# One-hots of picked experts laid out token by token, made by small VectorE operations

## The chip, the cores and the metric

The kernel runs on one core of one Trainium2 chip. The time is the device time of one execution in microseconds; lower is better. The core's engines work side by side, each through a queue of its own in a fixed order: TensorE (PE; its weight loads are listed as PEld), VectorE (DVE), ScalarE (ACT), GpSimd (POOL), and SyncE (SP), which issues transfers.

## What is computed

The reference is a transformer block with a mixture of 16384 experts (PEER), followed by two layers of another block, for 256 tokens of width 1024. The change touches the experts alone:

```python
def one(xb):                                  # xb: 128 tokens x 1024
    q = (xb @ w_pq).reshape(PEER_BLOCK, PEER_HEADS, 2, PEER_DKH)
    s = jnp.einsum('thpd,hpkd->thpk', q, sub_keys).astype(jnp.float32)
    sv, si = lax.top_k(s, PEER_TOPK)
    cand = (sv[:, :, 0, :, None] + sv[:, :, 1, None, :]).reshape(PEER_BLOCK, PEER_HEADS, -1)
    cidx = (si[:, :, 0, :, None] * N_KEYS + si[:, :, 1, None, :]).reshape(PEER_BLOCK, PEER_HEADS, -1)
    best, pos = lax.top_k(cand, PEER_TOPK)
    eidx = jnp.take_along_axis(cidx, pos, axis=-1)
    g = jax.nn.softmax(best, axis=-1)
    act = jax.nn.gelu(jnp.einsum('thkd,td->thk', expert_u[eidx], xb).astype(jnp.float32), approximate=False)
    return jnp.einsum('thk,thkd->td', (g * act).astype(xb.dtype), expert_v[eidx])
```

An expert's number is a pair (i, j) of two numbers under 128. Each token picks 16 of them in each of 8 heads, so 128 pairs with a weight each.

## The kernel before

The kernel gathers nothing. It computes all 16384 experts for all tokens, one slice of 128 experts (all i of one j) at a time, and multiplies the result by the tokens' weights, which are zero nearly everywhere. `up(j, lo)` is such a slice: a raw weight tile of 128x1024 is loaded, ScalarE copies it into `wh` (line 289), the high part, VectorE subtracts to get `wl` (line 293), the low part, and 24 matmuls follow in `mm3` (lines 274 to 276): for each of 8 parts of the model width `wh` with the tokens' high part, `wh` with their low part, `wl` with their high part. The first two of each three need `wh` alone. In this stage `wh` and `wl` have two buffers each (`wtile`, line 306).

The weights become a table by one-hots. For one token, partition p holds its p-th pick; `oo` is 1 in the column of the pick's i, `ow` holds the pick's weight in the column of its j, and the matmul of `oo` and `ow` sums over picks into a 128x128 table of that token. The weight is scaled by `WS` and split into two f16 parts, h = 0 and 1, so each token takes two matmuls. `prepare(t0)` makes `oo` and `ow` for four tokens, a group; `group()` does their eight matmuls (through `mm`, line 279) into one PSUM bank; `drain()` (lines 929 to 935) multiplies the finished slices `H1`, `H2` by the table, and ScalarE stores the table where no slice has come yet (line 935). In the loop at the end of this part, 64 groups are spread over 82 slices (`GR`), a group is prepared one ahead (`PD`), and drained three later (`LAG`). Where tokens already have their table, the slice's gelu (line 976) is multiplied into it (line 977).

`oo`, `ow` and the small tiles `k1` share six buffers (tag `k2`). The order of instructions on each engine is set by a scheduler when the program is built; each engine then keeps it. `choose` ends with the transposes that bring the picks' indices (`IJ`) and weights (`W2`) to partitions, a column per token.

Of the kernel before, what the change touches and what calls it, by code (L numbers as in the profile page):

```python
# [9 lines left out]
F32 = mybir.dt.float32  # L10
F32R = mybir.dt.float32r
BF = mybir.dt.bfloat16
F16 = mybir.dt.float16
U32 = mybir.dt.uint32
AF = mybir.ActivationFunctionType
OP = mybir.AluOpType
# [3 lines left out]
P = 128  # L20
D = 1024
T = 256
# [10 lines left out]
WS = 16384.0  # L33
# [226 lines left out]
class Kern:  # L260
# [566 lines left out]
    def peer(self, ys, gb):  # L827


        nc, tc, I = self.nc, self.tc, self.I  # L830
        st = ExitStack()
        pool = st.enter_context(tc.tile_pool(name="pe", bufs=1, reuse_waits="tile"))
# [11 lines left out]
            nc.sync.dma_start(xs[:, i * 512:(i + 1) * 512], self.X[i])  # L844
        nt.close()
        self.xpool.close()
        IJ = pool.tile([P, 2, T], F16, name="IJ")
        W2 = pool.tile([P, 2, T], F16, name="W2")
        io32 = pool.tile([P, P], F32, name="io32")
        nc.sync.dma_start(io32, I["iota"])  # L850
        iota = pool.tile([P, P, 4], F16, name="iota")
        nc.vector.tensor_copy(iota, io32[:, :, None].to_broadcast([P, P, 4]))
        g1s = st.enter_context(tc.tile_pool(name="g1", bufs=1, reuse_waits="tile"))
        H1 = g1s.tile([P, NJ1, T], F32, name="H1")
        tk = ExitStack()
        tp = tk.enter_context(tc.tile_pool(name="tk", bufs=1, reuse_waits="tile"))
# [18 lines left out]
        def second():  # L875
            ch = self.choose(tp, SV, SI, IJ, W2)
            for hp in range(16):
                w = pre
                if hp:
                    w = self.wsplit(self.raw(I["w_pq"][hp // 2], hp % 2, KD), lo="pool" if hp in POOLQ else "dve")  # L880
                pq = self.bank()
                for k in range(KD):
                    self.mm3(pq[:, :T], w[:, k], hT[k], k == 0, k == KD - 1)
                q = tp.tile([P, T], F32, tag="pq", name="pq", bufs=2)
                nc.scalar.activation(q, pq[:, :T], AF.Copy)
                yield
                sc = self.bank()
                for b in range(2):
                    self.mm(sc[:, b * P:(b + 1) * P], q[:, b * P:(b + 1) * P], skey[:, hp])
                for b in range(2):  # L890
                    o = (hp % 2, hp // 2 * 2 + b)
                    self.top16(tp, sc[:, b * P:(b + 1) * P], SV[:, o[0], o[1]], SI[:, o[0], o[1]])
                if hp % 2:
                    yield
                    next(ch)
                if hp % 4 == 3:
                    yield
                    next(ch)
                    yield
                    next(ch)  # L900
            next(ch)
            self.rest = ch
# [22 lines left out]
        def drain():  # L925
            nonlocal toks
            pg, ts = pend.pop(0)
            pv = pg.rearrange("p (t j) -> p j t", t=4)
            nc.vector.scalar_tensor_tensor(H1[:, :, ts], pv[:, :NJ1], 1.0 / WS, H1[:, :, ts], op0=OP.mult, op1=OP.mult)
            m = cols - NJ1  # L930
            if m:
                nc.vector.scalar_tensor_tensor(H2[:, :m, ts], pv[:, NJ1:cols], 1.0 / WS, H2[:, :m, ts],
                                               op0=OP.mult, op1=OP.mult)
            if cols < NKEY:
                nc.scalar.activation(H2[:, m:, ts], pv[:, cols:], AF.Copy, scale=1.0 / WS)
            toks = ts.stop

        def prepare(t0):
            ts = slice(t0, t0 + 4)
            B = [P, P, 4]  # L940
            oo = pool.tile([P, 2, P, 4], F16, tag="k2", name="oo", bufs=6)
            ow = pool.tile([P, 2, P, 4], F16, tag="k2", name="ow", bufs=6)
            for i in (1, 0):
                nc.vector.tensor_tensor(oo[:, i], iota, IJ[:, i, None, ts].to_broadcast(B), op=OP.is_equal)  # L944
            for h in range(2):
                nc.gpsimd.tensor_tensor(ow[:, h], oo[:, 1], W2[:, h, None, ts].to_broadcast(B), op=OP.mult)  # L946
            ready.append((oo, ow, ts))

        def group():
            oo, ow, ts = ready.pop(0)  # L950
            pg = self.bank()
            for i in range(4):
                for h in range(2):
                    self.mm(pg[:, i * P:(i + 1) * P], oo[:, 0, :, i], ow[:, h, :, i], start=h == 0, stop=h == 1)
            pend.append((pg, ts))
            if len(pend) > LAG:
                drain()
# [11 lines left out]
        for j in range(NJ1, NKEY):  # L969
            while n < 64 and n * GR < (j + 1 - NJ1 - GD) * 64:  # L970
                prepare(4 * n)
                n += 1
            pa = up(j, "dve" if j % PLO else "pool")
            if toks:
                ga = K1([P, T], F32)
                nc.scalar.activation(ga[:, :toks], pa[:, :toks], AF.Gelu)
                nc.vector.tensor_tensor(Hj(j)[:, :toks], ga[:, :toks], Hj(j)[:, :toks], op=OP.mult)
            if toks < T:
                nc.scalar.activation(Hj(j)[:, toks:], pa[:, toks:], AF.Gelu)
            cols = j + 1  # L980
            while len(ready) > (PD if n < 64 else 0):
                group()
            if n == 64 and not ready and pend:
                drain()
            if toks == T and j >= NKEY - VP:
                part(order[len(parted)])
# [38 lines left out]

    def choose(self, tp, SV, SI, IJ, W2):

# [3 lines left out]
        nc = self.nc  # L1031
        n = 4 * TOPK
        io32 = tp.tile([P, TOPK, n], F16, name="io32")
# [6 lines left out]
        stairs, o = [], 0  # L1040
# [5 lines left out]
        for h in range(PH):  # L1046
            cand = tp.tile([P, 2, o], F32, tag="cand", name="cand", bufs=2)
            hb = slice(2 * h, 2 * h + 2)
            for a0, a1, w, at in stairs:
                B = [P, 2, a1 - a0, w]  # L1050
                v.tensor_tensor(cand[:, :, at:at + (a1 - a0) * w].rearrange("p b (a c) -> p b a c", c=w),
                                SV[:, 0, hb, a0:a1, None].to_broadcast(B),
                                SV[:, 1, hb, None, 0:w].to_broadcast(B), op=OP.add)
            for b in range(2):
# [11 lines left out]
            t, ab = T2("t", F32, 4), T2("ab", F16, 2)  # L1066
# [16 lines left out]
            eq = tp.tile([P, 2, TOPK, n], F16, tag="eq", name="eq", bufs=1)  # L1083
            B = [P, 2, TOPK, n]
            v.tensor_tensor(eq, ab[:, :, None, :].to_broadcast(B), io32[:, None].to_broadcast(B), op=OP.is_equal)
# [11 lines left out]
        B = [P, 2 * PH, TOPK]  # L1097
# [11 lines left out]
        for b in range(2):  # L1109
            pt = self.bank()  # L1110
            for i in range(3):
                nc.tensor.transpose(pt[:, i * P:(i + 1) * P], ijw[:, i, b].rearrange("p h k -> p (h k)"), self.ident)
            o = slice(b * P, (b + 1) * P)
            nc.scalar.activation(IJ[:, :, o], pt[:, :2 * P].rearrange("p (i t) -> p i t", i=2), AF.Copy)
            pw = pt[:, 2 * P:3 * P]
            hi = tp.tile([P, P], F32, tag="whi", name="whi", bufs=2)
            nc.scalar.activation(W2[:, 0, o], pw, AF.Copy, scale=WS)
            nc.scalar.activation(hi, W2[:, 0, o], AF.Copy)
            nc.vector.scalar_tensor_tensor(W2[:, 1, o], pw, WS, hi, op0=OP.mult, op1=OP.subtract)
        yield  # L1120

    def glanes(self, *gens):
# [910 lines left out]
```

## Time and profile before

| | |
|---|---|
| median of 3 runs | 1929.62 us (1929.02 to 1930.05) |
| profiled execution | 1928.68 us |
| its span in the trace | 1926.9 us |
| mean granted TensorE clock | 0.992 of full speed |
| TensorE busy | 1857.6 us (96%) |
| VectorE busy | 1323.7 us (69%) |
| ScalarE busy | 970.3 us (50%) |
| GpSimd busy | 328.4 us (17%) |

Busy time is the time in which an engine has at least one instruction at work. The span is the profiled execution from its first to its last instruction; 1.8 us of the execution lie around it.

### The profile page before, as it was taken

Reading aid. Unit: us, or ns where it says so; the run is one execution under the profiler, and the core shown is the slowest. Engines: PE = TensorE matmul, PEld = TensorE weight load, DVE = VectorE, ACT = ScalarE, POOL = GpSimd, SP = SyncE. Lnnn points to the kernel's source line nnn. Section 1 sums busy time; section 2 is a strip of 40 time slices with the busy share of each in tenths; the row PEclk is TensorE's granted clock in tenths of the full one; section 3 lists DMA queues with packets and bytes.
Section 4 is the critical chain, followed back from the end, with each engine's and each line's share of the span. In section 5 each row is a group of like instructions: output and inputs, shape, how many; then the busy total and the mean of one; then the engine's idle time right before and its main releaser. Section 6 shows DMA issues by size and latency. Waiting matters only on the chain.

```text
span 1926.9 us, 32835 instructions
## 1 busy us (share of the span) xinstructions
PE 1857.6 (96%) x12634; PEld 1648.3 (86%) x12634; DVE 1323.7 (69%) x2901; ACT 970.3 (50%) x1792; POOL 328.4 (17%) x247
## 2 busy tenths in 40 slices
PE   7999989999999999999999999998999999989998
PEld 6776579999999999888888779987999899879997
DVE  4536668998788887555555665677777656767785
ACT  4535444443444444544444546445666464556563
POOL 0000003324644442000000003320100033200000
PEclk9999989999999999999999999999999999999999
DMA  8732544553444444656555653422666334225571
GB/s 309 246 109 89 175 144 141 177 174 122 148 138 142 143 142 154 209 190 189 187 186 184 208 195 110 131 66 82 200 223 228 100 110 132 66 77 172 194 232 60
DMA packets 85101, 302.93 MB, mean 157 GB/s; under 512 B 10096, under 2 KB 10992, under 8 KB 84816
## 3 DMA queue, kind: packets, MB, share of 16 engines
q1 hardware_dynamic: 84944, 300.83, 47.9%
q8 instruction: 99, 1.62, 0.4%
q14 instruction: 58, 0.48, 0.1%
HBM read 298.56 MB, written 2.10 MB: 156 GB/s over the span
## 4 chain that ended last, share of the span: by engine, by line
PE 78%; DVE 15%; ACT 3%; DMA 2%; issue 2%; SPq 0%; POOLq 0%; DVEq 0%; POOL 0%; ACTq 0%
PE b L276 20%; PE b L274 20%; PE b L275 20%; PE b L279 15%; DVE wl L293 4%; DVE oo L944 1%; PE b L1158 1%; ACT wh L289 1%; DMA raw<-in_wv 1%; PE b L524 1%; PE b L1349 1%; DVE eq L1089 0%; DVE tm L1022 0%; DVE u L1978 0%; DVE jt L741 0%
## 5 line engine op out<-in xcount | busy, mean ns | idle before, releaser
L289 ACT ACTIVATE wh<-raw 128x1024 fp32r<-128x1024 f32 x457 | 483.9, 1061 | 562.7 <-PE b L275 265.5
L293 DVE TENSOR_TENSOR wl<-raw,wh 128x1024 fp32r<-128x1024 f32 x414 | 559.7, 1352 | 270.8 <-ACT wh L289 270.5
L276 PE MATMUL b<-r,wl 128*128 128x256 f32 (+1 forms) x1216 | 347.5, 286 | 12.4 <-DVE wl L293 12.4
L274 PE MATMUL b<-r,wh 128*128 128x256 f32 (+1 forms) x1216 | 351.1, 289 | 0.0
L275 PE MATMUL b<-r,wh 128*128 128x256 f32 x1152 | 322.5, 280 | 0.0
L274 PE MATMUL b<-hh,wh 128*128 128x256 f32 x1056 | 301.6, 286 | 1.8 <-DVE ast L1674 1.8
L276 PE MATMUL b<-hh,wl 128*128 128x256 f32 x1056 | 299.7, 284 | 1.8 <-DVE wl L293 1.7
L275 PE MATMUL b<-hl,wh 128*128 128x256 f32 x1056 | 298.6, 283 | 0.0
L293 POOL TENSOR_TENSOR wl<-raw,wh 128x1024 fp32r<-128x1024 f32 x43 | 105.4, 2452 | 941.0 <-ACT wh L289 668.9
L276 PEld LDWEIGHTS b<-r,wl 128*128 128x128 f32 x1216 | 230.1, 189 | 21.3 <-DVE wl L293 19.8
L274 PEld LDWEIGHTS b<-r,wh 128*128 128x128 f32 x1216 | 231.2, 190 | 3.2 <-issue 1.5
L275 PEld LDWEIGHTS b<-r,wh 128*128 128x128 f32 x1152 | 218.3, 189 | 0.0
L274 PEld LDWEIGHTS b<-hh,wh 128*128 128x128 f32 x1056 | 202.2, 192 | 4.5 <-DVE ast L1674 2.3
L276 PEld LDWEIGHTS b<-hh,wl 128*128 128x128 f32 x1056 | 202.2, 191 | 3.1 <-DVE wl L293 3.0
L275 PEld LDWEIGHTS b<-hl,wh 128*128 128x128 f32 x1056 | 202.3, 192 | 1.4
L275 PE MATMUL b<-wl,k 128*128 128x512 f32 x492 | 195.0, 396 | 1.5 <-DVE wl L293 1.5
L274 PE MATMUL b<-wh,k 128*128 128x512 f32 x492 | 194.8, 396 | 0.0
L276 PE MATMUL b<-wh,k 128*128 128x512 f32 x492 | 194.6, 395 | 0.0
L946 POOL TENSOR_TENSOR ow<-oo,W 128x512 f16<-128x512 f16 x128 | 152.1, 1210 | 161.7 <-DVE oo L944 93.4
L275 PEld LDWEIGHTS b<-wl,k 128*128 128x128 f32 x492 | 92.4, 188 | 25.3 <-DVE wl L293 3.1
L1981 POOL TENSOR_TENSOR u<-u 128x256 f32<-128x256 f32 x44 | 33.6, 765 | 461.0 <-DVE u L1978 297.8
L274 PEld LDWEIGHTS b<-wh,k 128*128 128x128 f32 x492 | 92.4, 188 | 22.6 <-ACT wh L289 0.4
(491 smaller groups left out, 3150.4 us busy)
## 6 DMA issues: line engine op xcount, KB each, us to landing
raw<-in_eu SPq DMA_DIRECT2D x128, 512.0 KB, 3.9
raw<-in_ev SPq DMA_DIRECT2D x128, 512.0 KB, 3.6
raw<-in_fi SPq DMA_DIRECT2D x88, 512.0 KB, 4.5
raw<-in_w_ada SPq DMA_DIRECT2D x48, 512.0 KB, 5.3
raw<-in_wi SPq DMA_DIRECT2D x48, 512.0 KB, 3.9
raw<-in_fo SPq DMA_DIRECT2D x44, 512.0 KB, 4.6
raw<-in_w SPq DMA_DIRECT2D x16, 512.0 KB, 5.9
raw<-in_w_pq SPq DMA_DIRECT2D x16, 512.0 KB, 4.3
```

Source lines behind the costliest of these rows:

```text
L274: mm(out, L.hi, R.hi, start=start, stop=False, skip_group_check=True)
L275: mm(out, L.hi, R.lo, start=False, stop=False, skip_group_check=True)
L276: self.lastmm = mm(out, L.lo, R.hi, start=False, stop=stop, skip_group_check=True)
L279: self.nc.tensor.matmul(out, l, r, start=start, stop=stop, skip_group_check=True)
L289: nc.scalar.activation(dst.hi, src, AF.Copy)
L293: e.tensor_tensor(dst.lo, src, dst.hi.bitcast(F32), op=OP.subtract)
L524: nc.tensor.matmul(pa[32 * j:32 * j + 32, :P], self.s2[:, 4 * h + k], wa[:, k, m * P:(m + 1) * P], start=(k == 0), stop=(k == 3), tile_pos ...
L944: nc.vector.tensor_tensor(oo[:, i], iota, IJ[:, i, None, ts].to_broadcast(B), op=OP.is_equal)
L946: nc.gpsimd.tensor_tensor(ow[:, h], oo[:, 1], W2[:, h, None, ts].to_broadcast(B), op=OP.mult)
L1158: nc.tensor.matmul(pa[32 * j:32 * j + 32], self.s2[:, k], wa[:, j % 2 * 512:(j % 2 + 1) * 512], start=(k == 0), stop=(k == KD - 1), tile_p ...
L1349: nc.tensor.transpose(pt[:, sc * P:(sc + 1) * P], Pm[:, sc * P:(sc + 1) * P], self.ident)
L1981: nc.gpsimd.tensor_tensor(u[:, 0], u[:, 0], u[:, 1], op=OP.mult)
```

## The change

`oo` and `ow` are laid out token by token: the 128 columns of one token are neighbours, where before the four tokens of a group alternated. `oo` then holds the one-hot of i alone. `ow` is made straight from the column numbers in one operation with two per-partition scalars (equal to j, times the weight), where before a one-hot of j was made on VectorE and multiplied on GpSimd. Each operation covers one token, so a group takes 4 + 8 operations of 128 elements on VectorE, and none on GpSimd. `IJ` and `W2` become f32, and `iota` loses its factor of four.

```diff
-        IJ = pool.tile([P, 2, T], F16, name="IJ")
-        W2 = pool.tile([P, 2, T], F16, name="W2")
+        IJ = pool.tile([P, 2, T], F32, name="IJ")
+        W2 = pool.tile([P, 2, T], F32, name="W2")
...
-        iota = pool.tile([P, P, 4], F16, name="iota")
-        nc.vector.tensor_copy(iota, io32[:, :, None].to_broadcast([P, P, 4]))
+        iota = pool.tile([P, P], F16, name="iota")
+        nc.vector.tensor_copy(iota, io32)
...
         def prepare(t0):
             ts = slice(t0, t0 + 4)
-            B = [P, P, 4]
-            oo = pool.tile([P, 2, P, 4], F16, tag="k2", name="oo", bufs=6)
-            ow = pool.tile([P, 2, P, 4], F16, tag="k2", name="ow", bufs=6)
-            for i in (1, 0):
-                nc.vector.tensor_tensor(oo[:, i], iota, IJ[:, i, None, ts].to_broadcast(B), op=OP.is_equal)
-            for h in range(2):
-                nc.gpsimd.tensor_tensor(ow[:, h], oo[:, 1], W2[:, h, None, ts].to_broadcast(B), op=OP.mult)
+            oo = pool.tile([P, 4, P], F16, tag="k2", name="oo", bufs=6)
+            ow = pool.tile([P, 4, 2, P], F16, tag="k2", name="ow", bufs=6)
+            for i in range(4):
+                t = slice(t0 + i, t0 + i + 1)
+                nc.vector.tensor_scalar(oo[:, i], iota, IJ[:, 0, t], None, op0=OP.is_equal)
+                for h in range(2):
+                    nc.vector.tensor_scalar(ow[:, i, h], iota, IJ[:, 1, t], W2[:, h, t], op0=OP.is_equal, op1=OP.mult)
             ready.append((oo, ow, ts))
...
-                    self.mm(pg[:, i * P:(i + 1) * P], oo[:, 0, :, i], ow[:, h, :, i], start=h == 0, stop=h == 1)
+                    self.mm(pg[:, i * P:(i + 1) * P], oo[:, i], ow[:, i, h], start=h == 0, stop=h == 1)
...
-            hi = tp.tile([P, P], F32, tag="whi", name="whi", bufs=2)
-            nc.scalar.activation(W2[:, 0, o], pw, AF.Copy, scale=WS)
-            nc.scalar.activation(hi, W2[:, 0, o], AF.Copy)
-            nc.vector.scalar_tensor_tensor(W2[:, 1, o], pw, WS, hi, op0=OP.mult, op1=OP.subtract)
+            hi = tp.tile([P, P], F16, tag="whi", name="whi", bufs=2)
+            nc.scalar.activation(hi, pw, AF.Copy, scale=WS)
+            nc.scalar.activation(W2[:, 0, o], hi, AF.Copy)
+            nc.vector.scalar_tensor_tensor(W2[:, 1, o], pw, WS, W2[:, 0, o], op0=OP.mult, op1=OP.subtract)
```

The scheduler orders the changed program anew. On TensorE before, in the middle of the loop, with buffer numbers in the names (a slice has one `b`, `wh` and `wl`; `r` holds the tokens): the slice `b_6740` ends, the eight matmuls of a group follow, then the slice `b_6787` from its first matmul on.

```order
L276 MATMUL b_6740<-r_2441,wl_6737 128x256
L279 LDWEIGHTS oo_6675 [waits Activation_49]
L279 MATMUL b_6769<-ow_6676,oo_6675 128x128 [waits Pool_49]
...
L274 MATMUL b_6787<-r_2434,wh_6783 128x256 [waits Activation_49]
L275 MATMUL b_6787<-r_2434,wh_6783 128x256
L276 MATMUL b_6787<-r_2434,wl_6784 128x256 [waits DVE_49]
L274 MATMUL b_6787<-r_2435,wh_6783 128x256
```

On TensorE in the changed program, at the like place: the slice `b_6717` ends and a group follows; then come the first two matmuls of `b_6825`, the slice after next, and behind them the next slice, `b_6778`, whose own first two stand ahead of that group already.

```order
L276 MATMUL b_6717<-r_2441,wl_6714 128x256
L279 LDWEIGHTS oo_6697 [waits PE_49,DVE_49]
L279 MATMUL b_6807<-ow_6698,oo_6697 128x128 [waits Activation_49]
...
L274 MATMUL b_6825<-r_2434,wh_6821 128x256 [waits Activation_49]
L275 MATMUL b_6825<-r_2434,wh_6821 128x256
L276 MATMUL b_6778<-r_2434,wl_6775 128x256 [waits DVE_49]
L274 MATMUL b_6778<-r_2435,wh_6774 128x256
```

So two matmuls of each slice have moved ahead of the last 22 of the slice before it.

On ScalarE in the changed program, around the copy `wh_6821` that those two matmuls read: it waits for TensorE, and the gelu of the slice `b_6717` and the drain's store come behind it. The kinds stand in the same order as before the change.

```order
L935 ACTIVATE H2_4843<-b_6467 128x58x4 [waits DVE_49]
L289 ACTIVATE wh_6821<-raw_6819 128x1024 [waits DMAHW0_49,PE_49,Activation_49]
L976 ACTIVATE k1_6742<-b_6717 128x92 [waits PE_49,Activation_49]
L979 ACTIVATE H2_4843<-b_6717 128x164
L935 ACTIVATE H2_4843<-b_6528 128x57x4 [waits DVE_49]
```

On VectorE in the changed program, the same stretch: between two splits now stand the twelve small operations of a group, with L977 and L932 among them, where before two operations of L944 stood.

```order
L293 TENSOR_TENSOR wl_6775<-raw_6772,wh_6774 128x1024 [waits DMAHW7_49,DVE_49,PE_49]
L944 TENSOR_SCALAR oo_6758<-iota_2622,IJ_2618 128x128 [waits PE_49]
L977 TENSOR_TENSOR H2_4843<-k1_6742,H2_4843 128x92 [waits Activation_49]
L932 SCALAR_TENSOR_TENSOR H2_4843<-b_6528,H2_4843 128x35x4 [waits Activation_49]
L946 TENSOR_SCALAR ow_6759<-iota_2622,IJ_2618,W2_2619 128x128 [waits DVE_49]
...
L944 TENSOR_SCALAR oo_6758<-iota_2622,IJ_2618 128x128
L946 TENSOR_SCALAR ow_6759<-iota_2622,IJ_2618,W2_2619 128x128 x2
L929 SCALAR_TENSOR_TENSOR H1_2627<-b_6624,H1_2627 128x36x4
L293 TENSOR_TENSOR wl_6822<-raw_6819,wh_6821 128x1024 [waits DMAHW0_49,DVE_49,PE_49]
```

The multiplication L977 stands behind a split and ahead of the group's small operations, and it waits for ScalarE.

## Rows read from the trace of the kernel before

**Rows 1.** The page's chain that ended last, shares of the span by engine.

```profile
PE 78%; DVE 15%; ACT 3%; DMA 2%; issue 2%; SPq 0%; POOLq 0%; DVEq 0%; POOL 0%; ACTq 0%
```

**Rows 2.** Busy time by stretch: PE, PEld, DVE, ACT, POOL, then clock and DMA.

```profile
448.00:754.00 306.00, 302.79 (x2497) 293.24 (x2496) 249.48 (x412) 135.44 (x306) 152.13 (x128) 1.00 0.43 140
```

**Rows 3.** Groups by line and form, 448 to 752 us: busy, mean, idle ahead.

```profile
L946 POOL TENSOR_TENSOR ow<-oo,W 128x512 f16<-128x512 f16 x128 | 152.1, 1210 | 161.7 <-DVE oo L944 93.4 <-DVE H L977 42.6 <-ACT H L935 25.8
L293 DVE TENSOR_TENSOR wl<-raw,wh 128x1024 fp32r<-128x1024 f32 x81 | 134.7, 1663 | 0.8 <-ACT wh L289 0.8
```

**Rows 4.** Chain in order of time, 430 to 780 us: start, length, work.

```profile
473.52 0.95 PE b L279 x8
477.30 0.95 PE b L279 x8
481.07 0.96 PE b L279 x8
487.69 0.95 PE b L279 x8
...
575.73 0.96 PE b L279 x8
...
579.75 0.96 PE b L279 x8
...
586.60 0.97 PE b L279 x8
```

**Rows 5.** Timeline, 579.3 to 583.3 us: start, length, instruction, idle time ahead.

```profile
578.81 2.06 DVE L293 TENSOR_TENSOR wl<-raw,wh 128x1024 fp32r<-128x1024 f32 x1
...
579.59 1.11 PE L279 MATMUL b<-ow,oo 128*128 128x128 f16 x8
579.72 1.07 ACT L289 ACTIVATE wh<-raw 128x1024 fp32r<-128x1024 f32 x1 [1.56 <-PE b L275]
...
580.69 0.23 ACT L976 ACTIVATE k<-b 128x96 f32<-128x96 f32 x1
...
580.92 0.39 PE L276 MATMUL b<-r,wl 128*128 128x256 f32 x1
...
581.00 1.21 DVE L293 TENSOR_TENSOR wl<-raw,wh 128x1024 fp32r<-128x1024 f32 x1
...
582.13 0.24 DVE L977 TENSOR_TENSOR H<-k,H 128x96 f32<-128x96 f32 x1
...
582.30 0.29 DVE L932 SCALAR_TENSOR_TENSOR H<-b,H 128x144 f32<-128x144 f32 x1
...
582.52 0.41 DVE L944 TENSOR_TENSOR oo<-iota,IJ 128x512 f16<-128x512 f16 x1
```

**Rows 6.** Waits, 448 to 752 us: total, times, longest.

```profile
ACT wh L289 <- PE b L275: 76.4, 62, 3.5
...
PEld b L276 <- DVE wl L293: 9.3, 33, 1.0
```

**Rows 7.** Tile oo: shortest, median, longest in ns, first and last start.

```profile
L279 PE MATMUL b<-ow,oo x512: 283/297/303, 454.2 to 750.0; 128*128 128x128 f16 x171
L944 DVE TENSOR_TENSOR oo<-iota,IJ x128: 406/414/1277, 448.9 to 746.0; 128x512 f16<-128x512 f16 x128
```

**Rows 8.** VectorE's timeline at four places: runs of one operation, start and length.

```profile
280.04 0.48 DVE L783 TENSOR_TENSOR r<-h,r 128x128 fp32r<-128x128 f32 x2
280.44 0.72 DVE L782 TENSOR_SCALAR h<-b,a,mod 128x128 f32<-128x128 f32 x2
448.86 0.76 DVE L944 TENSOR_TENSOR oo<-iota,IJ 128x512 f16<-128x512 f16 x2 [2.45 <-ACT IJ L1114]
1171.89 1.25 DVE L1768 TENSOR_SCALAR gu<-klowupi,dgg 128x128 f32<-128x128 f32 x6
```

**Rows 9.** Busy time by stretch, as rows 2, of matmuls over 512 columns alone.

```profile
800.00:850.00 50.00, 50.00 (x215) 40.23 (x215) 27.70 (x37) 24.57 (x36) 0.00 (x0) 1.00 0.59 187
```

## The prediction

> **What bounds the kernel now.** I read the page's chain first: most of the span ends on TensorE's work [rows 1], so a saving on another engine counts only where TensorE waits for it. Then I looked at the stretch from 448 to 754 us, the only one where one-hots are made. TensorE is busy for 302.79 of 306 us at a granted clock of 1.00, VectorE for 249.48, GpSimd for 152.13 [rows 2]. By lines, VectorE's split `wl` takes 1663 ns a time here, and GpSimd is busy with `ow` alone [rows 3].
>
> The chain in order of time then shows the rhythm. I call one up-projection of 24 matmuls a slice, the eight one-hot matmuls a group, and from one group to the next a step. A step with one slice takes 473.52 to 477.30, 3.78 us, and one with two slices 481.07 to 487.69, 6.62 us [rows 4]. A group's chain piece is 0.95 to 0.96 us, so 0.119 us per one-hot matmul; a slice is 6.62 - 3.78 = 2.84 us, 0.118 us per matmul. Later the same steps take 4.02 and 6.85 us [rows 4]: there the split was 2.06 us long and TensorE's L276 started 0.05 us behind its end, 580.87 to 580.92 [rows 5]. The waits agree: L276's weight load waited 33 times for `wl`, 9.3 us [rows 6].
>
> The first group starts at 454.2 [rows 7], and the last two, which stand together, at about 748.3 (the last matmul starts at 750.0), so 294 us for 62 steps. The order of the program has 46 steps with one slice and 16 with two. Unstalled they would be 46 x 3.78 + 16 x 6.62 = 280 us; some 14 us are stalls on VectorE.
>
> **GpSimd goes, and with it VectorE's long splits.** The 128 operations on GpSimd leave. When GpSimd is idle a split is followed by the next VectorE instruction after 1.13 us (581.00 to 582.13) [rows 5], against a mean of 1.66 us now [rows 3]. All 14 us of stalls could go.
>
> **What VectorE gets.** Per group two operations over 512 elements leave, and twelve over 128 come: four with one per-partition scalar (`oo`), eight with two (`ow`), 768 in all. I price them by distances from start to start, since neighbours overlap. A two-input f32 operation takes 0.20 us over 128 elements (0.48 - 0.28, L783) [rows 8] and 1.13 over 1024: so 0.067 fixed and 1.04 ns per element. Over f16 the pair of L944 gives 0.76 - 0.42 = 0.34 us for 512, that is 0.53 ns per element, half. With two scalars L782 takes 0.72 - 0.40 = 0.32 us for 128 f32 elements from PSUM: 0.067 + 0.133 leaves 0.12, so 0.06 for each scalar. With one scalar and SBUF alone L1768 takes (1.25 - 0.27) / 5 = 0.196: less 0.127 that is 0.54 ns per element, half of the two-input rate.
>
> No row has a one-input f16 operation. Its stream of 128 elements lies between 0.133 us (as L783), 0.069 (as L1768) and 0.035 (L1768's halved, as f16 halved L783's rate). I take 0.035, since f16 did halve the rate in L944: 0.16 us with one scalar, 0.22 with two, 4 x 0.16 + 8 x 0.22 = **2.40 us per group**. At 0.069 it is 2.83, at 0.133 it is 3.60.
>
> [...]
>
> The rest of a step on VectorE is read off [rows 5]: split 1.13, L977 0.17 (582.13 to 582.30) growing with its tile, so 0.20; L932 0.22 growing, so 0.25; L929 as L932 at its smallest, 0.22. A step with one slice needs 2.40 + 1.80 = **4.20 us**, one with two 5.53.
>
> **What TensorE gets.** The one-hot matmuls read neighbouring columns where they read every fourth. The ends for one are 0.119 us as now and, by 512-column f32 matmuls (50 us for 215, 0.233 each [rows 9]), 128 columns at that rate: 0.058. It is closer to the latter in access, but its weight load has no row; I take 0.07. [...]
>
> **Where the order puts a new wait.** This is the step on which I lean most. Now the order is slice, group, slice. In the changed program nearly every group from the tenth on is followed by the first two matmuls of the slice *after next*, and only then come the 22 that remain of the next one. Those two need `wh` of the slice after next. `wh` has two buffers, so ScalarE can start that copy only when the slice that has just ended gives its buffer back. The copy starts at 579.72, 0.13 behind the group's start at 579.59, and takes 1.07 us [rows 5]; 62 such copies waited for L275 now [rows 6], at no cost, since the slice that needs them is a whole slice away. With 0.05 us to pass it on, the two matmuls can't start before 1.25 us behind the slice's end. The group fills 0.5 to 0.95 us of that, whatever it costs, and behind the two in the queue stand the 22 matmuls, which are ready. So a step with one slice takes 1.25 + 2 x 0.118 + 22 x 0.118 = **4.08 us** instead of 3.78. With two slices, the pair waits likewise, most of the group (about 6.5 of 8 matmuls) comes behind it, then twice 22: 1.25 + 0.24 + 6.5 x 0.07 + 44 x 0.118 = **7.13 us** (7.06 at 0.058, 7.45 at 0.119).
>
> **The sum.** TensorE alone: 46 x 4.08 + 16 x 7.13 = 301.8, less 5 early steps in the old order x 0.30 = 300.3 us, 6 more than 294. VectorE's 4.20 is over 4.08 in the 46 short steps, up to 5.5 us more, of which the slack in the long ones (7.13 - 5.53) can't be worked off ahead, because VectorE's queue stands at L977 until ScalarE has done the copy and then the gelu (0.97 us behind the copy's start [rows 5]). I take 4 of the 5.5. At the start VectorE makes three groups ahead of the next split in either order, six L944 of up to 1.28 us now [rows 7] and 36 x 0.2 = 7.2 us then; I count nothing for it. The changes to IJ, W2 and iota are a few operations once, beside a ScalarE that is busy for 135 of 306 us [rows 2]. So +10 us on the profiled execution's 1928.7, which lies 0.9 below the median of 1929.6: **1939.5 us**. With all uncertain prices at their cheap ends +5; with matmuls at 0.119 and all 5.5 it is +17.
>
> **Rivals.** About 0.2%, 4 us, is what a measurement of this kernel can tell from no change.
>
> *Faster: the pair's copy is there in time.* Should the copy for the slice after next be finished by the time the group ends, steps fall to VectorE's own need, 46 x 4.20 + 16 x 5.53 = 282 us: -12, 1918 us. If the small operations were cheaper too, TensorE's 46 x 3.40 + 16 x 6.24 = 256 would be the floor, -38. For it: 31 us of one-hot matmul time (512 x 0.061) and 14 us of stalls are there to gain. Against it: the two buffers, and 62 copies that started on L275. It decides once the round trip is under the group's 0.56 us. Chance 0.16.
>
> *The small operations stream no faster than f32.* At 2.83 a group a short step is 4.63 us: 46 x 4.63 + 16 x 7.13 = 327, +33, 1963 us; at 3.60 it is 5.40, +68, 1998 us. For it: no row of the operation. Against it: L944's halving. [...] Chance 0.14.
>
> *The change cancels out.* The stalls that go and the pair's wait even out within 4 us, at the cheap ends of all prices. Chance 0.11.
>
> **Chances.** My forecast, +4 to +18, has 0.59. Its own range is 1933.5 to 1948. Range: from 1922, which leaves out most of the faster case, to 1958, which leaves out most of the f32-rate case, with some 2 in 10 outside. Faster 0.17, same 0.13, slower 0.70.
>
> **What would show it.** From one group to the next 4.1 to 4.2 us where one slice lies between and about 7.1 where two do; TensorE's L274 waiting for `wh` of L289, some 0.3 to 0.7 us behind most groups, a wait that is absent now; splits back at 1.2 us; L944 and L946 together about 150 us from start to start; one-hot matmuls 0.06 to 0.08 us apart. I am wrong if short steps are under 3.9 us (no wait on `wh`), or if TensorE waits mainly for `wl` and `ow` with steps over 4.5 us (the small operations are dearer).

## The result, and the profile after

The changed kernel takes 1960.68 us (median of 4 runs, 1956.98 to 1962.66), the kernel before 1929.32 beside it: a ratio of 1.0162, 95% interval 1.0145 to 1.018. It is 31 us slower, where 10 were forecast. The profiled execution of it took 1962.66 us (span 1960.5).

First the tile view of the one-hots [rows 7]: shortest, median, longest duration in ns, first and last start.

```profile
L279 PEld LDWEIGHTS <-oo x512: 95/98/101, 456.8 to 779.6; 128*128 128x128 f16 x171
L279 PE MATMUL b<-ow,oo x512: 216/219/231, 456.8 to 779.8; 128*128 128x128 f16 x171
L944 DVE TENSOR_SCALAR oo<-iota,IJ x256: 236/247/264, 451.4 to 779.0; 128x128 f16<-128x128 f16 x128
```

The matmuls start 2.6 us later than before and end 30 us later. So most of the loss lies between the first and the last group; I call that stretch the stage. Below is its busy time, of before in the first fence and of the changed kernel in the second (columns as in [rows 2], now cut at the first and the last one-hot matmul).

```profile
454.20:750.00 295.80, 292.59 (x2411) 283.06 (x2409) 241.50 (x400) 130.91 (x294) 147.36 (x124) 1.00 0.43 141
```

```profile
456.70:779.80 323.10, 279.69 (x2415) 260.06 (x2413) 288.06 (x1021) 130.80 (x294) 0.00 (x0) 0.99 0.40 130
```

TensorE's busy time fell by 13 us and it now has 43 us in which it does nothing; before it was 3. VectorE is busy for 288 us of 323. The waits of the changed kernel from 448 to 785 us say what both stand for [rows 6]: total, times, longest.

```profile
ACT wh L289 <- PE b L275: 127.3, 63, 7.3
...
PEld b L274 <- ACT wh L289: 38.2, 43, 1.6
DVE H L977 <- ACT k L976: 31.5, 19, 3.8
PE b L274 <- ACT wh L289: 30.1, 38, 1.4
...
PEld b L276 <- DVE wl L293: 18.0, 21, 2.7
PE b L276 <- DVE wl L293: 13.2, 19, 2.4
```

The forecast wait of L274 on the weight copy is there, 43 times, and of TensorE's own 43 us it has 30.1, the split's L276 13.2. By this view alone the copy would be the cause; the first experiment tests that. What was not forecast is the third row as a cost: VectorE stands 31.5 us at L977, that is, it waits there for another engine while the work behind it in its queue can't pass. With its 288 us of work that is 319.5 of 323.1. And the kernel before had the same row, which the prediction did not count:

```profile
DVE H L977 <- ACT k L976: 30.7, 16, 2.1
```

One place shows how the stand reaches TensorE. The timeline of the changed kernel, behind a step with two slices (start, length, instruction, idle time ahead):

```profile
609.50 0.24 DVE L944 TENSOR_SCALAR oo<-iota,IJ 128x128 f16<-128x128 f16 x1
...
609.66 0.31 DVE L946 TENSOR_SCALAR ow<-iota,IJ,W 128x128 f16<-128x128 f16 x1
...
610.37 1.06 ACT L289 ACTIVATE wh<-raw 128x1024 fp32r<-128x1024 f32 x1 [2.18 <-PE b L275]
...
611.34 0.24 ACT L976 ACTIVATE k<-b 128x112 f32<-128x112 f32 x1
...
611.61 0.28 DVE L977 TENSOR_TENSOR H<-k,H 128x112 f32<-128x112 f32 x1 [1.64 <-ACT k L976]
...
612.19 0.53 DVE L946 TENSOR_SCALAR ow<-iota,IJ,W 128x128 f16<-128x128 f16 x2
...
613.85 1.22 DVE L293 TENSOR_TENSOR wl<-raw,wh 128x1024 fp32r<-128x1024 f32 x1
...
614.99 0.26 DVE L977 TENSOR_TENSOR H<-k,H 128x112 f32<-128x112 f32 x1
...
615.12 0.39 PE L276 MATMUL b<-r,wl 128*128 128x256 f32 x1 [0.54 <-DVE wl L293]
```

VectorE has done two small operations of the next group at 609.97 and then comes to L977, which needs ScalarE's gelu. ScalarE begins the weight copy at 610.37, when TensorE has read the last of that buffer, and the gelu only behind it. VectorE stands 1.64 us, works off the ten small operations that are left, and only then makes the split for which TensorE waits at L276.

### The profile page after: what moved, and what is told of

It is laid out like the page before. It is cut to its first block, busy times and chain, and to the rows that moved or that the text cites. A ratio compares the mean times of both kernels' runs of the same rounds, so it can differ in the third digit from the quotient of the medians.

```text
span 1960.5 us, 33290 instructions
## 1 busy us (share of the span) xinstructions
PE 1848.5 (94%) x12634; PEld 1629.4 (83%) x12634; DVE 1371.9 (70%) x3541; ACT 970.4 (49%) x1792; POOL 176.3 (9%) x119
## 4 chain that ended last, share of the span: by engine, by line
PE 51%; DVE 5%; ACT 2%; issue 1%; DMA 1%; POOLq 0%; POOL 0%; DVEq 0%; ACTq 0%
PE b L274 14%; PE b L276 14%; PE b L275 14%; PE b L279 7%; DVE wl L293 1%; ACT wh L289 1%; DVE u L1978 0%; DVE u L1605 0%; PE b L1875 0%; ACT jj L724 0%; DVE r L747 0%; DVE jt L741 0%; DMA raw<-in_wi 0%; PE b L1703 0%; DVE aE L1683 0%
## 5 line engine op out<-in xcount | busy, mean ns | idle before, releaser
L293 DVE TENSOR_TENSOR wl<-raw,wh 128x1024 fp32r<-128x1024 f32 x414 | 523.9, 1266 | 274.0 <-ACT wh L289 273.6
L274 PE MATMUL b<-r,wh 128*128 128x256 f32 (+1 forms) x1216 | 355.7, 293 | 30.1 <-ACT wh L289 30.1
L276 PE MATMUL b<-r,wl 128*128 128x256 f32 (+1 forms) x1216 | 347.6, 288 | 22.6 <-DVE wl L293 22.4
L274 PE MATMUL b<-hh,wh 128*128 128x256 f32 x1056 | 301.6, 286 | 1.8 <-DVE ast L1674 1.8
L276 PE MATMUL b<-hh,wl 128*128 128x256 f32 x1056 | 299.6, 284 | 1.8 <-DVE wl L293 1.7
L274 PEld LDWEIGHTS b<-r,wh 128*128 128x128 f32 x1216 | 233.0, 192 | 42.7 <-ACT wh L289 38.2
L276 PEld LDWEIGHTS b<-r,wl 128*128 128x128 f32 x1216 | 232.3, 192 | 30.2 <-DVE wl L293 28.5
L274 PEld LDWEIGHTS b<-hh,wh 128*128 128x128 f32 x1056 | 202.2, 191 | 4.6 <-DVE ast L1674 2.3
L276 PEld LDWEIGHTS b<-hh,wl 128*128 128x128 f32 x1056 | 202.2, 191 | 3.1 <-DVE wl L293 3.0
L274 PE MATMUL b<-wh,k 128*128 128x512 f32 x492 | 194.7, 396 | 0.0
L276 PE MATMUL b<-wh,k 128*128 128x512 f32 x492 | 194.6, 395 | 0.0
L946 DVE TENSOR_SCALAR ow<-iota,IJ,W 128x128 f16<-128x128 f16 x512 | 137.8, 307 | 0.0
L274 PEld LDWEIGHTS b<-wh,k 128*128 128x128 f32 x492 | 92.4, 188 | 22.5 <-ACT wh L289 0.2
L276 PEld LDWEIGHTS b<-wh,k 128*128 128x128 f32 x492 | 92.4, 188 | 22.2
```

What stands on the lines that cost most here:

```text
L274: mm(out, L.hi, R.hi, start=start, stop=False, skip_group_check=True)
L276: self.lastmm = mm(out, L.lo, R.hi, start=False, stop=stop, skip_group_check=True)
L293: e.tensor_tensor(dst.lo, src, dst.hi.bitcast(F32), op=OP.subtract)
L946: nc.vector.tensor_scalar(ow[:, i, h], iota, IJ[:, 1, t], W2[:, h, t], op0=OP.is_equal, op1=OP.mult)
```

## The experiments

Theory 1: VectorE comes last, 1a because its stands add to its work, 1b because something else paces it. Theory 2: TensorE's new order is the cost. Times are medians, with the ratio to the kernel before on the same chip; "the run in the old order" is the first experiment.

**TensorE's order undone.** The slices and groups are tied in the order slice, group, slice; VectorE's and ScalarE's orders stay but for a few neighbours that change places.

```diff
-            return self.upmm(w, hT, self.bank()[:, :T])
...
+            with tc.issue_after(self.lastmm.ins):
+                return self.upmm(w, hT, self.bank()[:, :T])
...
-                    self.mm(pg[:, i * P:(i + 1) * P], oo[:, i], ow[:, i, h], start=h == 0, stop=h == 1)
+            with tc.issue_after(self.lastmm.ins):
...
+                        self.lastmm = nc.tensor.matmul(pg[:, i * P:(i + 1) * P], oo[:, i], ow[:, i, h],
+                                                       start=h == 0, stop=h == 1, skip_group_check=True)
```

> The changed kernel with TensorE held to the order of the kernel before (slice, group, slice); VectorE's, ScalarE's and GpSimd's work stays as changed. Theory 1 (VectorE's own work decides): it is busy 272.7 of 306 us in the changed kernel, so about 288 of the 323 us from first group to last, and it stands at L977 besides; with the pair's wait gone the stage falls by no more than 4 to 20 us, 1941 to 1957 us. Theory 2 (the pair's wait for the weight copy, with the lateness that it hands to VectorE, decides): the stage falls to VectorE's 4.20 us in 46 short steps and TensorE's 6.24 in 16 long ones, 293 us, or to 282 if VectorE can work ahead: 1919 to 1931 us, and the waits on L289 and on the split are gone.

Measured: 1952.18 us, 1.0124 (1.0107 to 1.0141). The stage is 315.6 us, 7.5 less than in the changed kernel, and its waits from 448 to 800 us no longer have L274; they have the split instead, more than before:

```profile
PEld b L276 <- DVE wl L293: 55.2, 59, 2.8
...
DVE H L982 <- ACT k L981: 24.0, 18, 1.7
```

(L982 is L977 in this file. In the files of the runs in the old order L932 and L935 are the drain's two halves on VectorE, L929 and L932 of the changed kernel; below, L977 is the changed kernel's line, L932 and L935 are those of the runs.) So, with the stand in place, undoing the new order gives back a small part of the loss, and VectorE is the engine that comes last: theory 1.

**VectorE relieved.** In the same order, `ow` gets the high part alone and the matmuls read it twice (the low part is left out, and the high one counted twice).

```diff
-                for h in range(2):
-                    nc.vector.tensor_scalar(ow[:, i, h], iota, IJ[:, 1, t], W2[:, h, t], op0=OP.is_equal, op1=OP.mult)
+                nc.vector.tensor_scalar(ow[:, i, 0], iota, IJ[:, 1, t], W2[:, 0, t], op0=OP.is_equal, op1=OP.mult)
...
-                    self.mm(pg[:, i * P:(i + 1) * P], oo[:, i], ow[:, i, h], start=h == 0, stop=h == 1)
+                    ... oo[:, i], ow[:, i, 0], ...
```

> The same TensorE order, and the low part of the routing weights is left out: its one-hots aren't made (4 VectorE operations with two scalars fewer per group, 4 x 0.223 us), the matmuls read the high part's twice, so TensorE's work is unchanged and the result is less exact. Theory 1 (VectorE decides): 64 x 0.89 = 57 us less for it, so the stage falls towards TensorE's floor of 256 us, 1893 to 1905 us. Theory 2 (the order was the whole cost, and VectorE has slack without it): within 5 us of the run in the old order with all operations.

Measured: 1908.13 us, 0.9897 (0.9881 to 0.9914), 44 us under the run in the old order, 3 above the range of theory 1. VectorE's busy time in the stage fell by 52.7 us (286.79 to 234.11) and the stage by 44.7: most of what VectorE is spared comes back as time. TensorE is then busy for 264.88 of 270.9 us, so there is little left to give back.

**The layout alone.** The kernel before, its operations of 512 elements now writing token by token.

```diff
-                nc.vector.tensor_tensor(oo[:, i], iota, IJ[:, i, None, ts].to_broadcast(B), op=OP.is_equal)
+                nc.vector.tensor_tensor(oo[:, i].rearrange("p t j -> p j t"), iota, IJ[:, i, None, ts].to_broadcast(B), op=OP.is_equal)
...
-                nc.gpsimd.tensor_tensor(ow[:, h], oo[:, 1], W2[:, h, None, ts].to_broadcast(B), op=OP.mult)
+                nc.gpsimd.tensor_tensor(ow[:, h], oo[:, 1], W2[:, h, ts, None].to_broadcast([P, 4, P]), op=OP.mult)
```

> The kernel before with the layout alone changed: its one-hots are made by the same two VectorE and two GpSimd operations of 512 elements, but lie token by token, so that the matmuls read neighbouring columns. TensorE's order is that of before. If the layout is what helps TensorE, a one-hot matmul goes from 0.119 to 0.055 us as in the changed kernel, 30 us for the 512, of which VectorE and GpSimd let through what they are early: 1900 to 1925 us. If writing with a stride of 256 bytes slows L944 from 0.34 us and L946 from 1.21 us to twice that, GpSimd needs 4.8 us a group and decides: 64 x 4.8 = 310 us, some 1945 us.

Measured: 2135.32 us, 1.1073 (1.1054 to 1.1091). Both expectations were far too low. From 456 to 958 us VectorE's operation takes 2758 ns on average, and over all 128 of them 2516 in the median, where the median was 414 [rows 7]:

```profile
L944 DVE TENSOR_TENSOR oo<-iota,IJ 128x512 f16<-128x512 f16 x126 | 345.1, 2758 | 0.0
```

Walked in the old order (the four tokens innermost, so written with a stride of 256 bytes), the old operation is far dearer than the small ones (2758 ns for 512 elements; those of the changed kernel take 247 and 307 for 128). An operation of 512 elements that walks the columns of one token after the other wasn't tried, so it isn't shown that the layout needs the small ones.

**The small operations alone**, writing every fourth element as before, in the old TensorE order (`oo[:, :, i]` and `ow[:, h, :, i]` instead of `oo[:, i]` and `ow[:, i, h]`).

> The small VectorE operations, none on GpSimd, but writing the layout of before (every fourth element), in the old TensorE order. It parts the two halves of the change: TensorE's one-hot matmuls back at 0.119 us, VectorE with 12 small operations a group. If a small operation costs the same with a stride of 8 bytes (0.16 and 0.22 us), VectorE needs 4.2 us a short step and TensorE 3.8, so by theory 1 the time is that of the run in the old order with neighbouring columns, within 10 us; by theory 2 it is 20 to 30 us above it, since TensorE's 30 us come back in full. If the stride costs the fast rate, a group is 2.83 us or more and the time 1960 to 1990 us.

Measured: 2041.26 us, 1.0581 (1.0563 to 1.0598), off every expectation. It doesn't settle the time, since VectorE's order came out differently: drains stand ahead of splits, and L932, the drain's first half, waits 64.4 us for TensorE's groups. What it shows is the price (from 456.8 to 862.9 us):

```profile
L949 DVE TENSOR_SCALAR ow<-iota,IJ,W 128x128 f16<-128x128 f16 x499 | 176.3, 427 | 0.0
...
L947 DVE TENSOR_SCALAR oo<-iota,IJ 128x128 f16<-128x128 f16 x249 | 91.1, 366 | 1.9 <-PE b L958 1.9
```

That is 120 ns longer each than with neighbouring elements (307 and 247 in the changed kernel).

**The stand moved.** In the old TensorE order, L977 is put behind the 12 small operations of the next group; then L935, the drain's second half, as well.

```diff
-                nc.vector.tensor_tensor(Hj(j)[:, :toks], ga[:, :toks], Hj(j)[:, :toks], op=OP.mult)
+                late.append((Hj(j)[:, :toks], ga[:, :toks]))
...
                 prepare(4 * n)
                 n += 1
+                if late:
+                    with tc.issue_after(self.small.ins):
+                        flush()
```

> As the run in the old TensorE order, but VectorE's multiplication L977 of a slice stands behind all 12 small operations of the next group instead of among them, so that its wait for ScalarE's gelu falls on finished work. In the run in the old order VectorE stood there 24.0 us, 18 times, nearly all behind steps of two slices. If VectorE's stand is what makes the splits late (theory 1a), that run's 1952 us fall by 20 to 24 us, to 1928 to 1933. If VectorE only waits elsewhere instead, for the weight copies of L289 (theory 1b: two buffers pace it whatever its order), the time stays within 5 us of 1952 and its wait on L289 grows from 10 to 30 us.

Measured: 1960.89 us, 1.0152 (1.0132 to 1.0172), and both theories missed it: no gain, and the intervals of the two runs overlap, so a loss isn't certain either. VectorE's waits in the stage show that the stand went to the next instruction that needs the gelu:

```profile
DVE H L935 <- ACT H L996: 15.7, 17, 1.7
DVE H L932 <- PE b L958: 14.6, 5, 4.7
```

> As the run with L977 late, and the second half of a group's drain, L935, stands behind the next group's small operations as well. In the run with L977 late, VectorE's stand moved from L977 (24.0 us to none) to L935 (none to 15.7 us, 17 times), and 14.6 us at L932 came with it; nothing was gained. If it's the stand itself that costs, whichever instruction has it (theory 1a), taking away the last place where VectorE can stand for a gelu brings the stage from 323 us to about 295, 1930 to 1938 us. If VectorE is paced from outside, by the two buffers or by TensorE's results, the idle time turns up again at L932 or at the split, and the time stays at 1948 to 1962 us (theory 1b).

Measured: 1984.42 us, 1.0287 (1.0269 to 1.0304), dearer still and outside both expectations. In its stage, 350.1 us, VectorE now waits at L932 (42.9 us) and at `oo` for TensorE's group (20.6 us). That the results that wait longer hold buffers of the pool from which `oo` comes is likely, but not shown. Also, behind a long step the small operations of two groups now stand ahead of the next split. The two runs moved the stand and put new waits beside it, so they can't say what it costs.

**A third weight buffer**, in the old TensorE order.

```diff
-NRAW = 6
+NRAW = 5
...
-        h = pool.tile([P, 1024], F32R, tag="wh", name="wh", bufs=bufs)
+        h = pool.tile([P, 1024], F32R, tag="wh", name="wh", bufs=4 if self.spool else 3)
```

> As the run in the old TensorE order (1952 us), with a third buffer for the weight copy of L289, paid for with one buffer less for the raw weights (5 for 6). If VectorE's own work and stands decide, nothing changes, since VectorE waits for that copy only 10 us: 1949 to 1955 us. If the loop over two buffers paces both engines (theory 1b), the copies run ahead and the time falls by 10 us or more.

Measured: 1934.16 us, 1.0026 (1.0016 to 1.0036), 18 us under the run in the old order, as theory 1b had it. But only 10.7 of it lies in the stage (304.9 us), 1.8 in an earlier start and the rest behind the stage; and VectorE's order changed too: the next split now stands ahead of the L977 that waits. The stand there has gone, and 17 us of waits for a free buffer of `wl` have come. Buffer and order aren't told apart here.

**No stand at all.** In the old TensorE order, L977 multiplies by an old column instead of the newest gelu, and the drain leaves the newest column out; operations and sizes stay.

```diff
-                nc.vector.tensor_tensor(Hj(j)[:, :toks], ga[:, :toks], Hj(j)[:, :toks], op=OP.mult)
+                nc.vector.tensor_tensor(Hj(j)[:, :toks], H1[:, 0, :toks], Hj(j)[:, :toks], op=OP.mult)
...
-                nc.vector.scalar_tensor_tensor(H2[:, :m, ts], pv[:, NJ1:cols], 1.0 / WS, H2[:, :m, ts],
+                q = max(m - 1, 1)
+                nc.vector.scalar_tensor_tensor(H2[:, :q, ts], pv[:, NJ1:NJ1 + q], 1.0 / WS, H2[:, :q, ts],
```

> As the run in the old TensorE order (1952 us), but nothing on VectorE depends on the newest gelu: L977 multiplies by an older column of H1 instead of the gelu just made, and the drain L935 leaves the newest column out. The operations and their sizes stay (one column less in L935); part of the product is thus not the kernel's. VectorE can't stand for ScalarE there any more: 24.0 us at that line in the run in the old order. If VectorE's work and its stand together make the stage (theory 1a), the stage falls from 315.6 to 288 to 293 us, the time to 1925 to 1931 us. If the stand is only what is left over by another limit (theory 1b), VectorE waits for the weight copies of L289 or for TensorE instead, and the time stays at 1946 to 1955 us.

Measured: 1929.88 us, 1.0001 (0.9992 to 1.0011): 22 us less, theory 1a. In the stage VectorE does the same work, and the time around it has gone (columns as above):

```profile
454.90:747.00 292.10, 270.84 (x2409) 258.79 (x2408) 285.45 (x1021) 123.59 (x292) 0.00 (x0) 0.99 0.43 143
```

VectorE's order changed with the edit: in a short step L977 and L932 now stand behind the small operations, and at a long step the two splits follow each other. But VectorE's stretch around a long step, from the start of the first of its two splits to the start of the next split behind them, holds the same operations in both runs. First the run in the old order, then this one:

```profile
518.64 1.21 DVE L293 TENSOR_TENSOR wl<-raw,wh 128x1024 fp32r<-128x1024 f32 x1
...
526.09 1.22 DVE L293 TENSOR_TENSOR wl<-raw,wh 128x1024 fp32r<-128x1024 f32 x1
```

```profile
515.62 2.34 DVE L293 TENSOR_TENSOR wl<-raw,wh 128x1024 fp32r<-128x1024 f32 x2
...
521.34 1.21 DVE L293 TENSOR_TENSOR wl<-raw,wh 128x1024 fp32r<-128x1024 f32 x1
```

That is 7.45 us with the stand, of which 1.39 are the stand itself, and 5.72 without it. On TensorE it shows one step later. The groups around the step behind that long one, in the same two runs:

```profile
525.43 0.62 PE L958 MATMUL b<-ow,oo 128*128 128x128 f16 x8
...
530.06 0.62 PE L958 MATMUL b<-ow,oo 128*128 128x128 f16 x8
...
533.90 0.62 PE L958 MATMUL b<-ow,oo 128*128 128x128 f16 x8
```

```profile
522.41 0.62 PE L959 MATMUL b<-ow,oo 128*128 128x128 f16 x8
...
525.76 0.62 PE L959 MATMUL b<-ow,oo 128*128 128x128 f16 x8
...
529.59 0.62 PE L959 MATMUL b<-ow,oo 128*128 128x128 f16 x8
```

The step behind the long one takes 4.63 us with the stand and 3.35 without; the next one takes 3.84 and 3.83. From the second long step on, all such steps take 4.57 to 4.98 us with it and 3.34 to 3.56 without: some 20 of the 23.5 us by which the stage is shorter.

The same edit in the changed kernel and in the kernel before:

> The same edit in the changed kernel itself, with TensorE's order left to the scheduler. VectorE stood 31.5 us there. By theory 1a the stage falls from 323.1 us by some 20 to 30 us, until the pair's wait on TensorE (300 us by the prediction's sum) is what is left: 1932 to 1942 us. By theory 1b it stays within 6 us of 1960.7.

Measured: 1948.67 us, 1.0106 (1.0089 to 1.0122), 12 us less, between the two theories. The stage is 312.2 us against 292.1 with the old TensorE order, so with the stand gone TensorE's new order costs 20 us. Stand and order thus cover each other: taken away alone they give back 10.9 and 7.5 us of the stage, together 31.0. L274 still waits 32 times, and VectorE now stands for the copy too:

```profile
PEld b L274 <- ACT wh L289: 25.4, 32, 1.3
...
DVE wl L293 <- ACT wh L289: 17.1, 11, 3.0
```

> The same edit in the kernel before. VectorE stands 30.7 us at L977 there too, but its work and stands are 241.5 + 30.7 = 272 us of 295.8, under TensorE's 292.6. If the stand costs only where VectorE is the later engine, it is worth little here: its 14 us of late splits at most, 1915 to 1930 us. If a stand always costs, 30 us: about 1900 us.

Measured: 1920.22 us, 0.9951 (0.9934 to 0.9967), 8.5 us less, inside the first range. The edit didn't do its work here: VectorE's order came out otherwise and 25.0 us of the stand turned up at the drain. So this run doesn't show what the stand cost in the kernel before, and not that it cost nothing.

**Work moved off VectorE.** Four operations per group, the low part, go to GpSimd; or to ScalarE, as the high part's one-hot times the ratio of low to high weight.

```diff
-                    nc.vector.tensor_scalar(ow[:, i, h], iota, IJ[:, 1, t], W2[:, h, t], op0=OP.is_equal, op1=OP.mult)
+                    (nc.gpsimd if h else nc.vector).tensor_scalar(ow[:, i, h], iota, ...)
```

```diff
...
+                self.small = nc.vector.tensor_scalar(ow[:, i, 0], iota, IJ[:, 1, t], W2[:, 0, t], op0=OP.is_equal, op1=OP.mult)
+                nc.scalar.activation(ow[:, i, 1], ow[:, i, 0], AF.Copy, scale=W2[:, 1, t])
```

> As the run in the old TensorE order, but the 4 operations per group for the low part of the weights are issued on GpSimd, one token each; VectorE keeps 8. VectorE has 57 us less, as in the run that left them out (1908 us), if GpSimd's small operations disturb nothing: 1905 to 1912. If GpSimd at work lengthens VectorE's splits as in the kernel before (a mean of 1.66 us there against 1.22 without GpSimd), 80 splits take some 35 us more and eat most of it: 1925 to 1945 us.

Measured: 1920.05 us, 0.9945 (0.9927 to 0.9963), between its two cases. The splits stay at 1222 ns with GpSimd at work. Against the run without the low part two things are new: GpSimd is late (TensorE waits 6.2 us for it), and VectorE's own small operations are longer, a mean of 332 ns for 307. That these make up the whole difference isn't shown.

> As the run in the old TensorE order, but the low part is made by ScalarE: the high part's one-hot times the ratio of the low weight to the high one, 4 copies of 128 elements with a scale per group. VectorE has 57 us less, ScalarE, busy for some 135 of 306 us, gets 64 x 4 x about 0.3 = 77 us more. If VectorE's sum decides and ScalarE has room: about the time of the run without the low part, 1905 to 1915 us. If the copies stand in ScalarE's queue ahead of the weight copy and the gelu that TensorE and VectorE wait for: 1920 to 1940 us, with the wait of the split on L289 and that of L977 on the gelu grown.

Measured: 1910.48 us, 0.9896 (0.988 to 0.9913), its first case, as if the low part were free, though a copy takes 401 ns and ScalarE is busy for 218 us of 275.

> Both of it: ScalarE makes the low part, and L977 stands behind the next group's small operations. If VectorE's stands add to its work, this is below the run with ScalarE alone by 10 to 20 us, 1888 to 1902 us; TensorE's own floor in this stage, 46 x 3.35 + 16 x 6.17 = 253 us against 315 in the old order, would give 1890. If two weight buffers pace the two engines instead, it is within 5 us of the run with ScalarE alone.

Measured: 1906.61 us, 0.988 (0.9864 to 0.9897); 3.9 us under the run with ScalarE alone, within the 5 of the second expectation, and the intervals overlap.

> The same, with the low part made by ScalarE. The run with L977 late and ScalarE's low part, 1906.6 us, has 16 us of stands left, 9.5 at L935 and 6.8 at L977. By theory 1a some 10 of them go: 1893 to 1899 us. By theory 1b, and since VectorE waits there 32.5 us for the weight copies of L289 anyway, it stays within 4 us of 1906.6.

Measured: 1899.95 us, 0.9838 (0.9822 to 0.9855), by the ratios 8 us under the last one and 1 us above the range of theory 1a. With less work on VectorE the delay of L977 and L935 brings 11 us (from 0.9896), where it cost 31 with VectorE full (1.0287 against 1.0124).

> As the run with L977 late and the low part on ScalarE (1906.6 us), with a third buffer for the weight copy and 5 for the raw weights. There VectorE's split waits 32.5 us for that copy, 36 times, and TensorE stands 18 us for the split. If these waits sit on the path, the stage falls by up to 18 us, 1889 to 1900 us; if the second buffer's loop is covered by slack of TensorE, it stays within 4 us of 1906.6.

Measured: 1892.93 us, 0.9801 (0.9785 to 0.9818), inside its first range and the best version: 2.0% under the kernel before. Against the run that it starts from (ScalarE's copies and L977 late), the stage is 6.8 us shorter, and 4 more lie behind the stage. The kernel before wasn't tried with a third buffer. TensorE is busy for nearly all of the stage:

```profile
454.10:718.80 264.70, 262.38 (x2409) 258.84 (x2408) 233.15 (x775) 214.74 (x544) 0.00 (x0) 0.99 0.48 158
```

## Why the prediction missed

**What left with GpSimd: right.** The splits are back at 1216 ns each (1663 on average before, [rows 3]), and the next VectorE instruction follows after 1.14 us (613.85 to 614.99; 1.13 in [rows 5]).

**The price of the small operations: right.** In the timeline above, `oo` is followed by `ow` after 0.16 us (609.50 to 609.66), and an `ow` by the next after 0.22 (a pair takes 0.53 at 612.19, one 0.31), the two numbers of the prediction. The rival that they stream no faster than f32 is refuted by its price, 2.83 us a group or more (4 x 0.16 + 8 x 0.22 = 2.40 here), though its time, 1963, is near the measured one. No run takes the 0.16 us apart into a fixed part, a scalar and a stream, so the 0.035 us that the prediction took for the stream stays an estimate.

**The price of a one-hot matmul: a little better than taken.** Eight take 0.62 us where nothing stalls them (the rows below), so (0.62 - 0.219) / 7 = 0.057 us each, beside the 0.058 that the prediction had as its cheap end; 0.07 was taken.

**The wait of the pair: right in kind and place, its worth too small.** L274 waits behind a group, and the short step between the two groups here is 4.07 us, where 4.08 was forecast:

```profile
612.84 0.56 PE L279 MATMUL b<-ow,oo 128*128 128x128 f16 x7
...
617.82 0.62 PE L279 MATMUL b<-ow,oo 128*128 128x128 f16 x8
...
619.06 0.39 PE L274 MATMUL b<-r,wh 128*128 128x256 f32 x1 [0.62 <-ACT wh L289]
...
621.89 0.62 PE L279 MATMUL b<-ow,oo 128*128 128x128 f16 x8
```

From 510 us on, the short steps that don't follow a long one take 4.07 to 4.23 us. The step ahead of the one shown, directly behind a long one and the stand, takes 4.98 (612.84 to 617.82), and such steps take 4.6 to 5.5. The prediction leant on the pair's wait most and put 6 us on it. With the stand in place, undoing the order gives back 7 us of 31; without the stand the order is worth 20, and the stage is then 312 us where TensorE's sum said 300. This term of the sum was thus mis-sized as well.

**The step that failed: VectorE's term in the sum.** The prediction compared VectorE's 4.20 us with TensorE's 4.08 in the short steps and its 5.53 with 7.13 in the long ones, and took 4 us for the difference. It knew that VectorE's queue stands at L977, and used that only to say that slack is lost. But the stand is part of the long step: 30.7 us in 16 waits before, 1.92 us each, so VectorE needs 5.53 + 1.92 = 7.45 us there, more than TensorE (the stretch measured above took 7.45 with the stand, 5.72 without). By that, 46 x 4.20 + 16 x 7.45 = 312 us against the 304 of the forecast, 8 more from a row that stood in the profile. The work itself is 288 us where 281.7 were reckoned, 6 more; the 5 that are left to 323 are within what TensorE's new order is worth beside it, which is argued, not measured apart. What the runs show is the stage: 323.1 us, 315.6 without the new order, 292.1 without the stand as well, and 270.9 in the old order with 53 us of VectorE's work left out and the stand in place.

**The start: counted at nothing, 2.6 us.** The first group stands at 456.8 instead of 454.2. In the other runs it stands anywhere from 451.3 to 458.2 us, so it isn't shown that the change moved it. From 448 to 450 us TensorE's granted clock was 0.50, with 0.36 us of work from 444 to 446; before, it was 1.00 there, with 0.76 us of work from 444 to 446. The changed kernel:

```profile
448.00:450.00 2.00, 2.00 (x11) 2.00 (x11) 0.00 (x0) 0.00 (x0) 0.00 (x0) 0.50 0.47 168
```

**The end: not thought of, 3.8 us.** Behind the last group TensorE waits 2.44 us for one more split (at 782.45) and then runs at a granted clock of 0.50 from 782.4 to 788 us, with 0.41 us a matmul for 0.28. No experiment took start or end apart.

**The rival on the other side** (the copy is there in time) fell with the 43 waits of L274. Its estimate of VectorE's need alone, 282 us, is near the 285.45 us that VectorE works in the run without a stand; with the stand gone and the old order, that kernel is still only level with the one before: TensorE works 22 us less in the stage (270.84 for 292.59) and VectorE 44 more (285.45 for 241.50), and the stage is 292.1 us for 295.8, 6.7 and 3.2 above the busier of the two.

## What to carry to other kernels

Before work is moved to an engine, add to its busy time the waits that its own queue order makes it stand through: here nearly the whole of them came back as time where that engine was the last one (23.5 us of 24.0), and a third where TensorE's order was the next limit (10.9 of 31.5). Per step, compare work plus stands, not work. The longest wait of the busiest engine need not be the cause: TensorE's 30.1 us for the copy were worth 7.5, and with them gone it waited for the split instead. Where a gain on the busiest engine is paid for by the second busiest, ask whether a third one with room can take a share: here, in the old TensorE order, ScalarE's four copies per group turned a loss of 1.2% into a gain of 1.0%, and with L977 late and a third weight buffer into one of 2.0%.

## What the hardware showed beside

- An f16 comparison of 512 elements written with a stride of 256 bytes takes 2516 ns in the median, where 414 was the median with neighbouring elements (GpSimd at work in both); one of 128 elements written with a stride of 8 bytes 366 ns, where it is 247.
- The same one-hot matmul and its weight load take 219 and 98 ns with neighbouring columns, 297 and 117 ns with every fourth; from start to start 0.057 us and 0.119.
- VectorE's f32 split takes a mean of 1663 ns in the stretch with GpSimd's 512-element operations [rows 3], 1217 with none on GpSimd, and 1222 beside GpSimd's small operations of one token (858 ns in the median).
